# Requesting output-projection rows together, starting the SSD half earlier, and turning the SSD diagonal in a hybrid decoder layer

## The chip, the core and the metric

The kernel runs on one core of one Trainium2 chip. The metric is device microseconds of one execution; lower is better. Times before are given as the median of three runs, and one more execution was taken with the hardware profiler. The core's engines run side by side and meet at semaphores: PE multiplies matrices (its weight loads, PEld, overlap its multiplications), DVE and POOL work elementwise, ACT evaluates functions and scaled copies, and SP's queue issues the DMAs. Matrix products accumulate in PSUM, eight banks of 128 partitions by 512 floats.

## The reference

One decoder layer over 16 learned meta tokens and 1024 real tokens, width 1024, in float32. Cut to what matters here:

```python
h = concatenate([meta, x], axis=1)
proj = rms_norm(h, mix_pre_g) @ w_in                     # z, xbc, dt_raw, q, k, v
y_ssd = ssd_mixer(z, xbc, dt_raw, ...)                   # 16 heads of 64, 2 groups, chunks of 128
y_sb = rms_norm(stick_breaking_attention(q, k, v), sb_norm_g)   # 16 heads of 64, 128-query blocks
h = h + rms_norm(concatenate([y_ssd, y_sb], -1) @ w_out, mix_post_g)
gu = rms_norm(h, ffn_pre_g) @ w_up
h = h + rms_norm((gelu(causal_dwconv(gu[..., :D_FF])) * gu[..., D_FF:]) @ w_down, ffn_post_g)
return h[:, 16:]

# inside ssd_mixer, per chunk:
y_diag = einsum('bgcls,bgjcls,bcsgjp->bclgjp', CB, Ldec, Xdt)
y_off  = einsum('bclgn,bcgjpn,bgjcl->bclgjp', Cc, prev, exp(Acs))
y = (y_diag + y_off + xs * d_skip) * silu(z);  rms_norm(y, norm_g)
```

## The kernel before

Products whose operands are split are done three times: each float32 operand is written as a high part and a low part, and PE multiplies high by high, high by low and low by high into the same PSUM bank. Small products (scores, transposes, the SSD pieces, the halo) run in plain float32, and one such product shows as two matmul records in the trace; a transpose shows as one.

The stages, in order:

1. **Head.** The nine token tiles (16 meta tokens, then eight of 128) are loaded, normalised (L213) and turned through PE, eight 128x128 transposes a tile in two halves (L219), into `xh` (an ACT copy, L221) and `xl` (a DVE subtraction, L222). Both halves take their PSUM bank from one tag, `tp`, which has two buffers.
2. **First projections.** `dt` (16 columns) and the B and C blocks of group 0 run over the three column chunks `CH` (348, 346, 346 tokens) interleaved, by `project_steps` (L155 to L166). For `dt` that is 8 blocks of the contraction times 3 products a chunk. Nine transposes bring `dt` to tokens (`tpd`, L390), and a chain of some twenty DVE operations (L401 to L424) makes the decay exponents. `decays()` (L427) multiplies them on PE with triangular matrices (`pz_ea`, `pz_de`, `pz_cd`) after two steps of the following `x` projections; the B block is turned to tokens later.
3. **SSD scan.** For each of two groups, nine chunks (one of 16 tokens, eight of 128) pass through `chunk_weights`, `chunk_outputs` and `chunk_store`, between steps of the remaining projections (`fill`). In `chunk_outputs`, eight products `em` (128x128, stationary) by `xdt` (64 columns, moving), one a head, make the diagonal part `yg` in token layout (L507); DVE adds it to `yo` (L508); the part from the carried state `yf` is added; `chunk_store` turns `yo` by four transposes (L525).
4. **Attention.** For eight head pairs `p` and eight query blocks `i`, `block_weights` makes scores on PE (`z`, L596), two sigmoids on ACT (L597, L598), a scan on DVE (L601) and products on POOL (L603); `block_turn` transposes (L617) and copies (L619); `block_mix` multiplies by the values (`av`, L631), where two 64-column stationaries write the two partition halves of one bank. PE's order is as written here, by hand. `block_turn` follows three blocks behind. Between these, PE takes steps of `fill`, the q, k and v projections of the later pairs, which is used up in pair 6.
5. **Output projection, SSD half.** `wout_steps` (L701) takes the eight 128x1024 row blocks of `w_out` one by one: load into the tag `wraw` (two buffers), scaled copy to `wh` on ACT (L717), `wl` on DVE (L718), and `halo_mm`, two float32 products of the two halo tokens into 2-partition strips of one bank (strips at partitions 0 and 32 for even `k`, 64 and 96 for odd). It runs two steps a block from pair 6, block 5, to pair 7, block 1. `ssd_half` (`first`) then gives one step a half token tile, 24 products each: sixteen steps, of which pair 7 takes one each in blocks 2 to 4 and two each in blocks 5 to 7. After the last block a drain loop takes one at each round.
6. **Output projection, stick-breaking half.** `second` repeats `wout_steps` for rows 8 to 15, one step for each step left of `first` and the rest after it. Then the normalisations, the feed-forward layer and its down projection follow; after block 8 of this half everything is ordered by hand.

Where the order isn't written by hand, it comes from a scheduler that reads the program's order and dependencies. `wraw` holds 128x1024 floats in two buffers, and `whi` and `wlo` the same in three (`WB`); all three tags serve every weight that is loaded.

Of the kernel before, what the change touches and what calls it, by code (L numbers as in the profile page):

```python
# [16 lines left out]
P = 128  # L17
# [34 lines left out]
def tile_layer(ctx: ExitStack, tc: tile.TileContext, x, meta, rows, parts,  # L52
# [148 lines left out]
    with tc.tile_pool(name="pre", bufs=3, side="right") as pre:  # L201
        gpre = row_bcast(pre, 0, D, "gpre")
        for i in range(NT + 1):
# [11 lines left out]
            for hf in range(2):  # L215
                tp = psum_tp(f"xtp{i}_{hf}")
# [87 lines left out]
    with tc.tile_pool(name="ssd", bufs=1, side="right") as sp:  # L304
# [68 lines left out]
        dtT = rp.tile([16, L + 3], F32, name="dtT", tag="rt", bufs=1)  # L373

        def dt_evac(acc, c0, n):
            nc.vector.tensor_copy(dtT[:, c0:c0 + n], acc[:16, :n])

        head = [project_steps(load_w(w_dt, 16, "dt"), 16, xh, xl, CH, dt_evac, "dt")]
# [8 lines left out]
        for i in range(NT + 1):  # L387
            nr = NM if i == 0 else P
            c0 = 0 if i == 0 else NM + (i - 1) * P
            nc.tensor.transpose(tpd[:nr, i * 16:(i + 1) * 16], dtT[:, c0:c0 + nr], ident[:16, :16])  # L390
# [46 lines left out]
        run(fill, 2)  # L437
        decays()
        tmp.close()
        run(fill, 2)  # L440
        bc[0][1][0]()
# [40 lines left out]
        def chunk_outputs(g, c, em, xdt, yo, prev):  # L482
# [22 lines left out]
            yg = psum_sd(f"yd{nm}").rearrange("p (h d) -> p h d", d=64)  # L505
            for h in range(8):
                mm(yg[:nr, h, :], em[:nr, h, :nr], xdt[:nr, h, :], start=True, stop=True)  # L507
            nc.vector.tensor_tensor(yo[:nr], yg[:nr], yo[:nr], op=ALU.add)  # L508
# [9 lines left out]
        def chunk_store(g, c, yo, zk):  # L518
# [5 lines left out]
            for b in range(4):  # L524
                nc.tensor.transpose(tp[:, b, :nr], yo2[:nr, b * P:(b + 1) * P], ident[:nr, :nr])  # L525
# [14 lines left out]
        def scan_steps(g):  # L540
# [3 lines left out]
            for c in range(NT + 1):  # L544
# [4 lines left out]
                chunk_store(g, c, yo, zk)  # L549
# [151 lines left out]
    def wout_steps(pool, half, gain, res, y0, acc):  # L701
# [8 lines left out]
        for k in range(8):  # L710
            wr = wp.tile([P, D], F32, tag="wraw", name=f"wor{nm}{k}")
            r0 = (8 * half + k) * P
            nc.sync.dma_start(out=wr, in_=w_out[r0:r0 + P, :])
# [72 lines left out]
    for p in range(8):  # L786
        for i in range(NT):
# [7 lines left out]
            run(first, int(p == 7 and i > 4))  # L795
# [6 lines left out]
            if p == 6 and i == 5:  # L802
# [5 lines left out]
                wsteps = wout_steps(w1pool, 0, ssd_g, wres, halo_y(w1pool, 0, ssd_g), halo)  # L808
# [823 lines left out]
```

## Time and profile before

| | us |
|---|---|
| median of 3 runs | 1834.47 (1833.14 to 1835.4) |
| the profiled execution, its time | 1832.72 |
| the profiled execution, its span | 1831.0 |

| engine | busy, us | share of the span |
|---|---|---|
| PE | 1758.9 | 96% |
| PEld | 1508.3 | 82% |
| DVE | 1060.3 | 58% |
| POOL | 858.5 | 47% |
| ACT | 829.0 | 45% |

PE's busy time is the union of its matmul records, which overlap in the pipeline, so the price of one matmul in a stream is the distance from its start to the next start, not its duration. The granted TensorE clock over the span is 0.989 of full speed. PE is idle for 72.1 us in all; what ended those idle times is listed in the view of waits.

### The profile page before, as it was taken

The page shows a single profiled execution, that of the slowest core. Times are in us where ns is not written, and L with a number is a line of the kernel's source. Part 1 is how long each engine was busy: PE and PEld are TensorE (multiplying, and loading weights), DVE is VectorE, ACT ScalarE, POOL GpSimd, SP SyncE. Part 2 cuts the span into 40 slices and gives each one's busy share as a digit, 9 for nine tenths or more (in the row PEclk, how much of TensorE's full clock was granted, in tenths as well). Part 3 has the DMA queues.
Part 4 walks back from the last instruction along what each step waited for, and adds up shares of the span by engine and source line. Part 5 has one row for each costly group of instructions (what it writes and reads, how often), then busy time and mean ns, then how long its engine had stood idle before and what let it go on. Part 6 is the DMA issues. An engine that isn't in the chain of part 4 may idle for free.

```text
span 1831.0 us, 27362 instructions
## 1 busy us (share of the span) xinstructions
PE 1758.9 (96%) x10957; PEld 1508.3 (82%) x10957; DVE 1060.3 (58%) x1142; ACT 829.0 (45%) x1371; POOL 858.5 (47%) x613
## 2 busy tenths in 40 slices
PE   6899999999999999999799989899999999999997
PEld 5899889889888888888478767788889998888886
DVE  5551783574534544544722256766666666667988
ACT  5333454443655655655654243443333333344444
POOL 3213563485644644643764132276777776600001
PEclk9999999999999999999899999999999999999999
DMA  4123242231011110110232455233233333196344
GB/s 155 47 70 119 75 125 96 71 103 54 24 36 36 32 39 28 32 36 11 82 106 70 139 175 181 81 104 92 87 103 111 104 103 99 52 316 230 95 120 160
DMA packets 91443, 173.96 MB, mean 95 GB/s; under 512 B 11722, under 2 KB 36714, under 8 KB 91316
## 3 DMA queue, kind: packets, MB, share of 16 engines
q1 hardware_dynamic: 91316, 172.21, 29.9%
q8 instruction: 86, 1.41, 0.3%
q14 instruction: 41, 0.34, 0.1%
HBM read 122.39 MB, written 49.79 MB: 94 GB/s over the span
## 4 chain that ended last, share of the span: by engine, by line
PE 47%; DVE 3%; ACT 2%; POOL 1%; issue 1%; DMA 1%; POOLq 0%; SPq 0%; ACTq 0%; DVEq 0%
PE dn L1445 11%; PE fX L1054 9%; PE mo L759 6%; PE fY L1054 6%; PE fA L1054 6%; PE tw L617 1%; PE av L631 1%; PE z L596 1%; PE pj_v L163 1%; PE pj_q L163 1%; PE halo L708 1%; PE pj_k L163 1%; DVE oxn L912 1%; DVE mb L903 1%; POOL yl L749 0%
## 5 line engine op out<-in xcount | busy, mean ns | idle before, releaser
L601 DVE TENSOR_TENSOR_SCAN kp<-kp,hold 128x272 f32<-128x272 f32 (+7 forms) x128 | 206.7, 1657 | 202.3 <-ACT kp L597 99.6
L603 POOL TENSOR_TENSOR bt<-bt,kp 128x256 f32<-128x256 f32 (+7 forms) x128 | 213.8, 1688 | 195.9 <-DVE kp L601 143.3
L997 POOL TENSOR_TENSOR wl<-wr,wh 128x1024 fp32r<-128x1024 f32 x44 | 110.7, 2524 | 40.7 <-ACT wh L996 40.7
L1445 PE MATMUL dn<-dl,dh 128*128 128x512 f32 x308 | 120.1, 390 | 0.1
L1445 PE MATMUL dn<-dh 128*128 128x512 f32 x308 | 120.1, 390 | 0.0
L1445 PE MATMUL dn<-dh,dl 128*128 128x512 f32 x308 | 120.0, 390 | 0.0
L1491 POOL TENSOR_TENSOR fms<-fms,nhalf 128x1 f32<-128x1 f32 x8 | 8.5, 1060 | 225.8 <-DMA ar<-fda 186.0
L597 ACT ACTIVATE kp<-z 128x288 f32<-128x288 f32 (+6 forms) x112 | 82.7, 738 | 60.4 <-PE z L596 37.3
L1374 ACT ACTIVATE dh<-ar 128x512 fp32r<-128x512 f32 x77 | 48.7, 632 | 111.2 <-PE dn L1445 88.9
L996 ACT ACTIVATE wh<-wr 128x1024 fp32r<-128x1024 f32 x44 | 46.6, 1060 | 114.9 <-PE fX L1054 68.3
L596 PE MATMUL z<-k,q 64*128 64x144 f32 (+6 forms) x448 | 88.0, 494 | 8.3 <-ACT bt L598 3.9
L1126 DVE SCALAR_TENSOR_TENSOR ga<-gr,pp,ga 128x1024 f32<-128x1024 f32 x44 | 71.4, 1622 | 34.7 <-ACT ga L1119 34.0
L619 ACT ACTIVATE th<-tw 128x1024 f32<-128x1024 f32 (+2 forms) x96 | 74.4, 811 | 33.2 <-PE tw L617 31.1
L598 ACT ACTIVATE bt<-z 128x288 f32<-128x288 f32 (+6 forms) x112 | 83.0, 741 | 0.0
L617 PE MATMUL tw<-ident,bt 128*128 128x128 f32 x576 | 78.3, 282 | 4.4 <-POOL bt L603 2.9
L631 PE MATMUL av<-th,v 128*64 128x128 f32 x1152 | 78.1, 281 | 0.0
L631 PEld LDWEIGHTS av<-th,v 128*64 128x64 f32 x1152 | 62.6, 138 | 18.1 <-issue 17.3
L1375 DVE TENSOR_TENSOR dl<-ar,dh 128x512 fp32r<-128x512 f32 x77 | 53.2, 691 | 41.9 <-ACT dh L1374 41.8
L617 PEld LDWEIGHTS tw<-ident,bt 128*128 128x128 f32 x576 | 62.9, 143 | 15.9 <-issue 10.6
L596 PEld LDWEIGHTS z<-k,q 64*128 64x128 f32 x448 | 37.8, 191 | 39.0 <-issue 15.8
L1445 PEld LDWEIGHTS dn<-dh 128*128 128x128 f32 x308 | 57.8, 188 | 12.3 <-ACT dh L1374 0.3
L1445 PEld LDWEIGHTS dn<-dl,dh 128*128 128x128 f32 x308 | 57.9, 188 | 12.2 <-DVE dl L1375 0.4
(542 smaller groups left out, 5797.1 us busy)
## 6 DMA issues: line engine op xcount, KB each, us to landing
wr<-in_w_up SPq DMA_DIRECT2D x44, 512.0 KB
fds<-ga SPq DMA_DIRECT2D x44, 256.0 KB
b<-in_w_down SPq DMA_DIRECT2D x44, 256.0 KB
ar<-fds SPq DMA_DIRECT2D x44, 256.0 KB
fda<-ga SPq DMA_DIRECT2D x33, 256.0 KB
ar<-fda SPq DMA_DIRECT2D x33, 256.0 KB
yk<-yd SPq DMA_DIRECT2D x16, 512.0 KB
zd<-zt SPq DMA_DIRECT2D x8, 520.0 KB
```

The source lines that it names most:

```text
L596: mm(z[:, j, :w], q[h, t0:t0 + P], k[h, a:a + w], start=True, stop=True)
L597: nc.scalar.activation(kp[:, :, a:a + w], z[:, :, :w], AF.Sigmoid, scale=-QSCALE)
L598: nc.scalar.activation(bt[:, :, a:a + w], z[:, :, :w], AF.Sigmoid, scale=QSCALE)
L601: nc.vector.tensor_tensor_scan(kp[:, j][:, ::-1], kp[:, j][:, ::-1], hold[:, L - n:L][:, ::-1], 0.0, op0=ALU.mult, op1=ALU.max)
L603: nc.gpsimd.tensor_tensor(bt[:, j, 0:m], bt[:, j, 0:m], kp[:, j, 1:m + 1], op=ALU.mult)
L617: nc.tensor.transpose(tw[:, j, b, :], bt[:, j, c0:c0 + P], ident)
L619: nc.scalar.activation(th[:, :, :nb, :], tw[:, :, :nb, :], AF.Copy)
L631: mm(av[halves[j], :], v[:, kb, halves[j]], th[:, j, b, :], start=kb == 0, stop=kb == i)
L759: mm(acc, u[:, k, :], v[:, cs], start=(k == 0 and j == 0), stop=(k == 7 and j == 2))
L997: nc.gpsimd.tensor_tensor(l, raw, h.bitcast(F32), op=ALU.subtract)
L1054: mm(acc[:, c, :nn], u[:, k, :], v[:, k, c0:c0 + nn], start=first and k == 0 and j == 0, stop=k == 3 and j == 2, skip_group_check=not first)
L1445: mm(banks[t], u[:, 0, c], v[:, 1, :], start=(p == 0 and i == 0), stop=(p == NPR - 1 and i == 2))
```

## The change

- **Head.** The half-tile transposes take their bank in turn from the tags `tp`, `z` and `sd`, of two buffers each.
- **dt.** The high and low parts of `w_dt` lie side by side as one 32-column stationary, which is multiplied with `xh` and `xl`: 16 products a chunk for 24, and a term low by low that was left out is now included. The two halves are added by the turn to tokens, a float32 product with a 32x16 matrix of two stacked identities (`fold`).
- **decays.** It comes after four steps of `fill` and after the turn of the B block.
- **SSD diagonal turned.** `xdt` (64 columns) is now stationary and `em` (128 columns) moving, so the diagonal part comes out with the channels on the partitions, two heads in the two halves of the bank, in `chunk_store`. The four transposes of `yo` accumulate onto it, and the DVE addition L508 is gone.
- **SSD half.** All eight raw row blocks are requested in block 4 of pair 6, two into `wraw` and six into `whi` and `wlo`; `wout_steps` runs four steps in block 5 and four in block 6; `first` begins in block 7 of pair 6 and then runs in blocks 1, 3, 5, 6 and 7 of pair 7, one step each.
- **Halo.** The halo products of two consecutive row blocks are issued together.
- **Second half.** Its eight raw row blocks are requested at once, four into `wraw` and four into a tag `wr` of three buffers; two steps of `second` follow each step of `first`; the second token tile is split before the loop.
- The scratch for dynamic DMA is set to 2048.

```diff
-                tp = psum_tp(f"xtp{i}_{hf}")
+                tp = (psum_tp, psum_z, psum_sd)[(2 * i + hf) % 3](f"xtp{i}_{hf}")
...
+        dtT = rp.tile([32, L + 3], F32, name="dtT", tag="rt", bufs=1)
+        fold = sp.tile([32, 16], F32, name="fold", tag="fold")
+        nc.vector.tensor_tensor(fold, ident[:32, 0:16], ident[:32, 16:32], op=ALU.add)
+        def dt_steps():
+            raw = wp.tile([P, KB, 16], F32, tag="wraw", name="wr_dt")
+            hl = wp.tile([P, KB, 32], F32R, tag="whi", name="wh_dt", bufs=WB)
+            nc.sync.dma_start(out=raw, in_=w_dt)
+            nc.scalar.activation(hl[:, :, 0:16], raw, AF.Copy)
+            nc.gpsimd.tensor_tensor(hl[:, :, 16:32], raw, hl[:, :, 0:16].bitcast(F32), op=ALU.subtract)
+            for c0, n in CH:
+                acc = psum_mm(f"pj_dt_{c0}")
+                for k in range(KB):
+                    for j, src in enumerate((xh, xl)):
+                        mm(acc[:32, :n], hl[:, k, :], src[:, k, c0:c0 + n],
+                           start=(k == 0 and j == 0), stop=(k == KB - 1 and j == 1))
+                nc.vector.tensor_copy(dtT[:, c0:c0 + n], acc[:32, :n])
+                yield
...
-            nc.tensor.transpose(tpd[:nr, i * 16:(i + 1) * 16], dtT[:, c0:c0 + nr], ident[:16, :16])
+            mm(tpd[:nr, i * 16:(i + 1) * 16], dtT[:, c0:c0 + nr], fold, start=True, stop=True)
...
-        run(fill, 2)
+        run(fill, 4)
+        bc[0][1][0]()
         decays()
         tmp.close()
-        run(fill, 2)
-        bc[0][1][0]()
         run(fill)
...
-            yg = psum_sd(f"yd{nm}").rearrange("p (h d) -> p h d", d=64)
-            for h in range(8):
-                mm(yg[:nr, h, :], em[:nr, h, :nr], xdt[:nr, h, :], start=True, stop=True)
-            nc.vector.tensor_tensor(yo[:nr], yg[:nr], yo[:nr], op=ALU.add)
...
             for b in range(4):
-                nc.tensor.transpose(tp[:, b, :nr], yo2[:nr, b * P:(b + 1) * P], ident[:nr, :nr])
+                for j in range(2):
+                    mm(tp[halves[j], b, :nr], xdt[:nr, 2 * b + j, :], em[:nr, 2 * b + j, :nr],
+                       start=b == 0, stop=False, skip_group_check=True)
+            for b in range(4):
+                mm(tp[:, b, :nr], yo2[:nr, b * P:(b + 1) * P], ident[:nr, :nr], start=False, stop=True,
+                   is_transpose=True, skip_group_check=True)
...
         for k in range(8):
-            wr = wp.tile([P, D], F32, tag="wraw", name=f"wor{nm}{k}")
-            r0 = (8 * half + k) * P
-            nc.sync.dma_start(out=wr, in_=w_out[r0:r0 + P, :])
+            wr = raws_.pop(0) if raws_ else raw_w(half, k, None)
...
             if len(todo) > 1:
-                halo_mm(*todo.pop(0))
+                for arg in todo:
+                    halo_mm(*arg)
+                todo.clear()
             yield
-        halo_mm(*todo.pop(0))
...
-            run(first, int(p == 7 and i > 4))
+            if p == 6 and i == 4:
+                ahead = [raw_w(0, k, None if k % 3 == 0 and k < 6 else wp_f32(("wlo", "whi", "wlo")[k % 3], f"wora{k}"))
+                         for k in range(8)]
...
-            if p == 7 and i == 1:
+            if p == 6 and i == 6:
                 run(wsteps)
                 halo_store(w1pool, 0, halo)
+                ys1 = [split_y(wp, 0, 1, ("whi", "wlo", WB))]
                 first = ssd_half(wres, ys1)
-            elif p > 5:
-                run(wsteps, 2)
-            if p == 7 and i == 0:
-                ys1 = [split_y(wp, 0, 1, ("whi", "wlo", WB))]
-            run(first, int(p == 7 and i > 1))
+            elif p == 6 and i == 5:
+                run(wsteps, 4)
+            run(first, int(p == 7 and (i % 2 or i > 5) or p == 6 and i == 7))
...
+    y0b = halo_y(op, 1, sb_g)
+    ahead = [raw_w(1, k, None if k % 5 < 2 else est.tile([P, D], F32, tag="wr", name=f"worb{k}", bufs=3)) for k in range(8)]
+    second = wout_steps(op, 1, sb_g, wres2, y0b, halo, ahead)
     run(second, 1)
     ys = [split_y(op, 1, 1, ("yh", "yl", 2))]
     for _ in first:
-        run(second, 1)
+        run(second, 2)
     run(second)
+    ys.append(split_y(op, 1, 2, ("yh", "yl", 2)))
...
-        if t < NT - 1:
+        if 1 < t < NT - 1:
             ys.append(split_y(op, 1, t + 1, ("yh", "yl", 2)))
...
-    nc = bacc.Bacc("TRN2", target_bir_lowering=False, num_devices=1)
+    nc = bacc.Bacc("TRN2", target_bir_lowering=False, num_devices=1, dynamic_dma_scratch_size=2048)
```

More of the change, by code (lines that the diff above doesn't have):

```diff
@@ L371, in tile_layer @@
         nc.scalar.activation(expa, alog, AF.Exp)
[L373 to L378, printed above, removed]
+        dtT = rp.tile([32, L + 3], F32, name="dtT", tag="rt", bufs=1)
[15 more added lines that the diff above has]
+                yield
+        head = [dt_steps()]
         bc = bc_flow(0)
@@ L516, in chunk_outputs, with chunk_store @@
             return yo, zk, nprev
-        def chunk_store(g, c, yo, zk):
+        def chunk_store(g, c, em, xdt, yo, zk):
             nr = NM if c == 0 else P
@@ L699, in attend_meta, with raw_w, wp_f32, wout_steps @@
         nc.gpsimd.tensor_copy(sq[:, M0:NM], sqm[:, 0, :])
-    def wout_steps(pool, half, gain, res, y0, acc):
+    def raw_w(half, k, tile_):
+        wr = tile_ if tile_ is not None else wp.tile([P, D], F32, tag="wraw", name=f"wor{half}{k}")
+        r0 = (8 * half + k) * P
+        nc.sync.dma_start(out=wr, in_=w_out[r0:r0 + P, :])
+        return wr
+    def wp_f32(tag, name):
+        return wp.tile([P, 8, P], F32R, tag=tag, name=name, bufs=WB).bitcast(F32).rearrange("p a b -> p (a b)")
+    def wout_steps(pool, half, gain, res, y0, acc, raws_):
         nm = "ab"[half]
```

9 lines of the change are left out of this document (4 added, 5 removed).

## The prediction

> **What bounds the kernel now.** I read the page's summary first, then the busy time of stretches of the span, then PE's own waits, and last the instructions of the stretches that the change touches.
>
> ```profile
> PE 1758.9 (96%) x10957; PEld 1508.3 (82%) x10957; DVE 1060.3 (58%) x1142; ACT 829.0 (45%) x1371; POOL 858.5 (47%) x613
> ```
>
> PE is busy 96% of the 1831.0 us, so its idle time is only 72.1 us. Next, where that lies (us from the start; after the total come PE, PEld, DVE, ACT and POOL busy, the granted clock, and the DMA share).
>
> ```profile
> 0.00:50.00 50.00, 32.35 (x184) 26.79 (x185) 25.20 (x44) 24.12 (x43) 14.23 (x24) 1.00 0.43 141
> 200.00:420.00 220.00, 213.62 (x1319) 192.90 (x1318) 147.05 (x174) 109.61 (x233) 127.35 (x108) 0.99 0.32 95
> 860.00:917.60 57.60, 45.35 (x364) 27.89 (x359) 40.94 (x28) 39.86 (x63) 36.70 (x26) 0.91 0.27 82
> 917.60:1030.00 112.40, 110.64 (x651) 86.19 (x652) 24.23 (x22) 47.79 (x76) 48.85 (x33) 1.00 0.30 94
> 1030.00:1068.00 38.00, 33.74 (x151) 20.59 (x150) 15.93 (x16) 15.25 (x20) 7.63 (x3) 1.00 0.49 154
> ```
>
> The idle time lies in the head (17.6 us), between the end of the projections and the first SSD output step (12.2 us, at a granted clock of 0.91) and around the second half's weights (4.3 us). The SSD scan, 200 to 420, is full of PE work: 6.4 us idle in 220. So two kinds of edit pay here: PE work taken out where PE is full, and idle time filled where it is not. What ends the idle times (total, times, longest, in us):
>
> ```profile
> PE xtp L219 <- DVE xl L222: 6.0, 4, 2.2
> PE pz_ea L431 <- DVE s L419: 4.9, 1, 4.9
> PE z L596 <- ACT bt L598: 3.9, 2, 3.5
> ```
>
> **The change part by part.**
>
> *SSD diagonal.* Now, and what has the turned form's shape:
>
> ```profile
> 233.28 1.02 PE L496 MATMUL st<-xw,bn 128*128 128x512 f32 x2
> 234.14 1.89 PE L507 MATMUL yd<-xdt,em 128*128 128x64 f32 x16
> 235.84 0.40 PE L163 MATMUL pj_X<-xh,wh_X 128*128 128x346 f32 x1
> ...
> 966.88 1.09 PE L631 MATMUL av<-th,v 128*64 128x128 f32 x16
> 967.91 1.31 PE L617 MATMUL tw<-ident,bt 128*128 128x128 f32 x10
> ```
>
> Eight products in the old form take PE from 234.14 to 235.84, 1.70 us. The turned form has 64-column stationaries, 128 moving columns, and two partition halves in turn. That is exactly `av`, whose eight products take 966.88 to 967.91, 1.03 us. With 16 full chunks this gives 16 x 0.67 = 10.7 us; the two 16-token chunks I leave at zero. The four transposes stay. None of them accumulates in this trace; the bounds are no cost and, if each ran as two records like other float32 products, the four once more, at most their whole duration:
>
> ```profile
> 242.84 0.60 PE L525 MATMUL yt<-ident,yo 128*128 128x128 f32 x4
> L508 DVE TENSOR_TENSOR yo<-yd,yo x18: 671/678/692, 193.2 to 433.2; 128x512 f32<-128x512 f32 x16, 16x512 f32<-16x512 f32 x2
> ```
>
> 0.60 us x 16 = 9.6 us at worst. I take none, since operation, operands and sizes stay. The DVE addition that goes (18 x 0.678 = 12.2 us of DVE time) counts nothing where PE leads; at best it takes some of the stage's 6.4 us of idle. Term: -10.7, from -14 to 0.
>
> A rule of the Trainium skill speaks against this edit: "TensorE: Matmul & The Clock Gate", section "Back-to-back issue gap", prices matmuls by moving columns, 60 cycles up to 64 and 134 at 128. By that ratio the turned set would be 134/60 x 1.70 = 3.8 us, an estimate from that page, and the kernel 16 x 2.1 = 34 us slower in this stage, some 1848 in all. The `av` row already disagrees: twice the moving columns of `yd` at 0.6 of the price.
>
> *dt.*
>
> ```profile
> 58.53 0.32 PE L163 MATMUL pj_dt<-xl,wh_dt 128*16 128x346 f32 x1
> 58.69 0.32 PE L163 MATMUL pj_dt<-xh,wl_dt 128*16 128x346 f32 x1
> 66.57 0.68 PE L390 MATMUL tpd<-ident,dtT 16*16 16x16 f32 x9
> 67.17 0.42 PE L163 MATMUL pj_X<-xh,wh_X 128*128 128x348 f32 x1
> ...
> 1043.17 2.07 PE L296 MATMUL ptb<-ones,sq 128*2 128x1 f32 x18
> ```
>
> 24 products fewer at 0.16 us are 3.8 us; the stationary grows from 16 to 32 columns, which I count as free, since the moving columns are the same. Nine plain products replace nine transposes: those take 0.60 us, and nine narrow float32 products with 128-row stationaries take 2.07 us, so 1.4 us more. Term: -2.4, from -3.8 (no extra) to -0.9 (the first chunk's third, 1.3 us, already hidden by DVE's tiles, and a little more).
>
> *Head.*
>
> ```profile
> 16.63 1.94 PE L219 MATMUL xtp<-ident,xn 128*128 128x128 f32 x8 [2.19 <-DVE xl L222]
> 20.64 1.94 PE L219 MATMUL xtp<-ident,xn 128*128 128x128 f32 x8 [2.07 <-DVE xl L222]
> 18.61 1.29 DVE L213 SCALAR_TENSOR_TENSOR xn<-xt,rs_pre,gpre 128x1024 f32<-128x1024 f32 x1 [1.20 <-PE xtp L219]
> 19.81 1.28 DVE L222 TENSOR_TENSOR xl<-xtp,xh 128x512 fp32r<-128x512 f32 x2
> ```
>
> A tile takes 4.0 us (16.63 to 20.64): PE waits for both banks until DVE's `xl`, and DVE then waits 1.20 us for PE to free `xn`. With six banks the transposes no longer wait; DVE's own 1.29 + 1.28 and some small ones, say 2.8 us, is late next. Three tiles pass before PE fills up with projections: 3 x 1.2 = 3.6 us, of the 6.0 us of this wait. Term: -3.5, from -6.0 to 0 (DVE leads anyway).
>
> *decays.* PE reaches `pz_ea` 4.9 us early; two steps of 24 x 0.16 = 3.8 us were meant to lie between, and about 13 us of work did.
>
> ```profile
> 71.51 0.15 DVE L401 TENSOR_TENSOR dtx<-tpd,dtb 16x16 f32<-16x16 f32 x1
> 85.27 0.31 DVE L419 SCALAR_TENSOR_TENSOR s<-dt,expa 128x144 f32<-128x144 f32 x1
> 88.72 0.49 PE L163 MATMUL pj_X<-xh,wh_X 128*128 128x348 f32 x1
> 89.59 0.49 PE L163 MATMUL pj_X<-xh,wh_X 128*128 128x348 f32 x1
> ```
>
> DVE's chain ends 19.0 us after the start of `tpd` (66.57 to 85.58). Four steps, the B turn (about 1.2 us) and the longer fold (2.0) put 18.5 us of PE work there: about 0.5 us of stall left, 4.4 us gained. After the stall three products take 0.87 us (88.72 to 89.59) instead of 0.48, for some 3 us; without the stall that goes too, about 1 us. Term: -5.0, from -6.5 to -2.5 (the scheduler may put it earlier again).
>
> *SSD half and its halo products.*
>
> ```profile
> 900.91 1.04 PE L708 MATMUL halo<-wora,y 128*2 128x512 f32 x8
> 906.13 1.03 PE L708 MATMUL halo<-wora,y 128*2 128x512 f32 x4 [0.60 <-DMA wora<-in_w_out]
> L708 PE MATMUL halo<-worb,y 128*2 128x512 f32 x32 | 7.2, 591 | 1.8 <-POOL yl L749 1.2 <-DMA worb<-in_w_out 0.6
> L708 PE MATMUL halo<-wora,y 128*2 128x512 f32 x32 | 7.0, 702 | 0.8 <-DMA wora<-in_w_out 0.8
> 889.03 3.71 DMA wora<-in_w_out
> 927.84 5.51 PE mo L759 x24
> SPq L713 <- PE halo L708: 32.2, 7, 10.2
> 864.00:901.00 37.00, 26.66 (x175) 15.14 (x177) 29.27 (x20) 27.31 (x43) 25.53 (x14) 0.86 0.20 58
> L718 DVE SCALAR_TENSOR_TENSOR wola<-wora,pp,woha 128x1024 fp32r<-128x1024 f32 x5 | 8.7, 1731 | 4.0 <-ACT woha L717 4.0
> ```
>
> Two row blocks in four strips cost 1.04 us, the price of one in two strips (1.03), so the strips run side by side. Eight blocks cost 7.0 us now and 4 x 1.04 = 4.2 in pairs: -2.8. The requests now wait 32.2 us on SP for `wraw`, and a row (3.71 us) then ends waits; with eight buffers, free by the end of the projections near 864, it does not. PE's idle time there has other causes too: the chain of ACT, DVE and POOL on bare blocks. DVE is busy 29.27 of 37 us in blocks 3 to 7 of pair 6 with five `wl`; eight add 3 x 1.73 = 5.2 us, 34.5 of 37, and ACT gets three more copies: DVE is late next, and I charge 2 us. One step of `first` (24 products, 5.5 us) then lies in block 7 and one in pair 7's block 1, and later blocks of pair 7 lose four of nine: blocks 0, 2 and 4 go bare, which I charge 1.5 us, against 1.8 us idle there now. Filling the early holes returns perhaps 3.7 of the 12.2 us. Term: -2.8 + 2 + 1.5 - 3.7 = -3.0, from -17 (all idle and clock loss of that stretch) to +9.
>
> *Second half.* It has the same halo saving, 7.2 us to 4.2, -3.0. Five steps of `first` (27 us) now cover eight rows at 3.7 us each and the split, where two did; the 4.3 us idle goes except 1.3. On SP, rows 5, 6 and 7 wait for a buffer, and the yk load and the stores of `first` are queued behind; the first pair frees `wraw` one step in, 5.5 us, and the second split is asked for before its use. Term: -6.0, from -7.3 to -1.
>
> The rest, normalisations, feed-forward and tails, has the same instructions and moves as a block; the scratch size counts nothing, because every data transfer is on a queue issued by SP. Sum: -10.7 - 2.4 - 3.5 - 5.0 - 3.0 - 6.0 = -30.6. The profiled execution took 1832.7, so 1802.1; the median lies 1.8 above it, so I give **1803**.
>
> **The rivals.**
>
> *The steps fill the whole hole.* All idle and clock loss of 860 to 917.6 (12.2 + 0.09 x 57.6 = 17.4 us) goes, 14 beyond my net 3: 1789. For it: ACT and DVE are near 70% there. Against: they and POOL wait on each other, and DVE gets more.
>
> *Bare blocks.* Blocks 0, 2 and 4 of pair 7 behave as blocks 3 to 7 of pair 6 do: 10.3 us idle and 0.14 x 37 = 5.2 us of clock over five blocks, so 9.3 for three, +9: 1812. For it: the same engines. Against: the small blocks have less to wait for. Part 1 of the same page says that an idle window of about 3.4 us halves the clock; the 0.86 row agrees.
>
> *The column halves follow each other.* Priced by `st`, 0.86 us (233.28 to 234.14) for two records of 512 columns, 16 records of 128 take 1.72 us; the diagonal gains nothing: 1814. Against: the `av` row.
>
> *Requests stay late*, so the change does not do what it says: SP holds the rows as now, and terms five and six go: 1812. Against: the buffers are free.
>
> *Slower.* In the turned form each record's price doubles with its moving columns: 1.70 to 3.40 us in the SSD scan, where nothing hides it. That is +27.2 in place of -10.7: 1841. It decides from a set of 2.95 us (19.9 us of other gains over 16 chunks). Against it, `av` at 1.03 with the same shapes; for it, only that the operands differ. The page rule above is this rival.
>
> **How the numbers follow.** Forecast 0.53; hole filled 0.13; bare blocks 0.17; halves in turn 0.08; requests late 0.04; slower 0.05. The range 1788 to 1816 takes in all but the slower case and the tails of the terms. A difference of 0.2% (3.7 us) is what a measurement can tell. Faster 0.93, same 0.02, slower 0.05.
>
> **What would show it.** Right: sixteen diagonal records in about 1.03 us and no L508; 48 `dt` products; no wait of `xtp` on `xl` and under 1 us at `pz_ea`; halo groups of eight records, four a half; no wait of `halo` or `mo` between the last block and the normalisations; pair 7 with 3 us idle or less. Wrong: a diagonal set near 1.7 or 3.4 us, or pair 7 with over 10 us idle or a granted clock under 0.9.

## The result, and the profile after

The changed kernel takes 1810.33 us (median of 4 runs, 1809.65 to 1811.43) against 1834.93 us (4 runs) for the kernel before beside it: a ratio of 0.9867, 95% interval 0.985 to 0.9884. That is 24.6 us faster; 31 were forecast, to 1803. The profiled execution has a span of 1809.0 us, 22.0 less than before.

The summary of the profile after, in the columns of the one before:

```profile
PE 1734.8 (96%) x10942; PEld 1490.1 (82%) x10942; DVE 1061.0 (59%) x1125; ACT 831.3 (46%) x1373; POOL 863.3 (48%) x613
```

PE's busy time fell by 24.1 us and its idle time rose, from 72.1 to 74.2. So the change took work out of PE, as planned; it did not fill holes. Where holes are now (total, times, longest, in us):

```profile
PE xtp L221 <- DVE ms_pre L188: 11.4, 1, 11.4
PE xtp L221 <- DVE xn L213: 6.5, 4, 4.3
PE z L612 <- ACT bt L614: 6.0, 3, 4.7
...
PE mo L783 <- ACT yh L772: 4.3, 1, 4.3
PE z L612 <- DVE thc L659: 4.1, 7, 2.3
PE tt_B L331 <- DVE bn L327: 2.9, 1, 2.9
...
PE mo L783 <- POOL yl L773: 2.4, 2, 1.7
...
PE halo L733 <- DMA worb<-in_w_out: 1.8, 1, 1.8
...
PE pz_ea L447 <- DVE s L435: 1.0, 1, 1.0
```

The wait of `xtp` on `xl` (6.0 before) has become one of 6.5 on `xn`; the 4.9 at `pz_ea` shrank to 1.0, with 2.9 new at the turn of B. `mo <- yh` grew from 0.9 to one wait of 4.3, `z <- bt` from 3.9 to 6.0 and `z <- thc` from 2.0 to 4.1. The stretches after, in the columns of before (head, scan, blocks 3 to 7 of pair 6, pair 7, the second half's rows):

```profile
0.00:50.00 50.00, 32.16 (x190) 29.53 (x191) 25.88 (x45) 24.03 (x44) 13.70 (x24) 0.93 0.42 142
200.00:420.00 220.00, 214.98 (x1415) 189.11 (x1415) 151.73 (x160) 110.83 (x231) 135.69 (x114) 1.00 0.33 98
841.00:885.00 44.00, 33.14 (x220) 20.26 (x218) 41.17 (x24) 36.00 (x57) 32.80 (x16) 0.92 0.23 73
885.00:985.00 100.00, 92.93 (x646) 71.53 (x644) 27.98 (x25) 44.51 (x72) 48.37 (x38) 0.98 0.18 57
985.00:1035.00 50.00, 42.24 (x187) 29.64 (x185) 12.62 (x13) 21.27 (x28) 11.91 (x5) 0.90 0.56 190
```

In the last blocks of pair 6 (841 to 885) DVE works 41.2 of 44 us and PE 33.1. Around the second half's rows PE is idle 7.8 us of 50 at a clock of 0.90.

To see where the time came from, the span is cut at six marks: the first `sg` (the scan begins), the last `yt` (it ends), the last `pj_v` (the projections end), the last `avc` (the attention ends), the first `x2tp` (the normalisations begin) and the last `dn`. Steps of `first` were moved past the last `avc`, three of them; at 5.5 us a step (the row of 24 `mo` records shown with the prediction) the table counts all kernels as if nine steps lay before it.

| stretch, us | before | after | difference | forecast |
|---|---|---|---|---|
| start to first `sg` (head, dt, decays) | 176.0 | 169.5 | -6.5 | -10.9 |
| to last `yt` (scan, diagonal) | 262.4 | 248.3 | -14.1 | -10.7 |
| to last `pj_v` | 425.2 | 423.6 | -1.6 | 0 |
| to last `avc` (attention, SSD half) | 158.6 | 144.1 + 16.5 | +2.0 | -3.0 |
| to first `x2tp` (second half) | 59.7 | 78.9 - 16.5 | +2.7 | -6.0 |
| to last `dn` (all the rest) | 738.6 | 734.1 | -4.5 | 0 |

The first three parts together gave 22.2 us where 21.6 were forecast, but not part by part: the head gave 4.4 less, the scan 3.4 more, and 1.6 came where nothing was changed. The two parts of the output projection, forecast at -9.0, cost 4.7.

Part of this scatter is the clock. Read in slices of 1 us, the granted clock is 1.00 or 0.50, but for the few slices that hold an edge between the two. The time at half clock in the six stretches is 6.8, 3.4, 3.4, 10.3, 0.0 and 10.3 us before and 13.6, 0.0, 0.0, 10.2, 10.2 and 3.4 after: always a multiple of some 3.4 us. Such a window of 3.4 us costs up to 1.7 us, and less where PE is idle in it. PE's idle time in the six is 24.1, 6.4, 1.5, 14.0, 4.3 and 11.8 us before and 21.8, 5.0, 1.5, 17.9, 8.2 and 9.7 after. So the -1.6 is one window, and the +2.0 of the attention is 3.9 us more idle time against less work. Up to the last `dn` the two executions are alike, 34.2 and 37.4 us at half clock.

What is behind the +2.7 stands in the timeline of the changed kernel around 1000 us (start, duration, engine, line; in brackets the idle time before and what ended it):

```profile
990.53 1.38 SPq L720 DMA_DIRECT2D worb<-in_w_out  x3
...
994.18 0.80 SPq L720 DMA_DIRECT2D wor<-in_w_out  x2
...
999.26 0.33 SPq L720 DMA_DIRECT2D worb<-in_w_out  x1
...
999.63 0.90 SPq L771 DMA_DIRECT2D yk<-yd  x2
...
1006.92 1.06 ACT L772 ACTIVATE yh<-yk 128x1024 fp32r<-128x1024 f32 x1 [0.46 <-DMA yk<-yd]
1008.03 1.22 PE L783 MATMUL mo<-woha,yh 128*128 128x512 f32 x2 [4.27 <-ACT yh L772]
...
1010.94 0.79 PE L783 MATMUL mo<-woha,yl 128*128 128x512 f32 x1 [1.69 <-POOL yl L773]
```

SP issues in order. Its last row waits until 999.26 for a buffer that the halo products free, and only then go out two loads `yk`, among them that of token tile 7, which the SSD half needs next; `yh` is made at 1006.92, and PE stands until 1008.03 and again until 1010.94. The theory for the experiments was therefore: the diagonal, `dt` and the head give what they give alone; the second half's loss is the order on SP's queue; the SSD half's is DVE, full where eight `wl` are now packed into blocks 5 and 6 of pair 6, and the bare blocks of pair 7. The rivals: transfers that collide for bandwidth, DVE that is busy but not late, and bare blocks alone.

### The profile page after: what moved, and what is told of

It is laid out like the page before. It is cut to its first block, busy times and chain, and to the rows that moved or that the text cites. A ratio compares the mean times of both kernels' runs of the same rounds, so it can differ in the third digit from the quotient of the medians.

```text
span 1809.0 us, 27308 instructions
## 1 busy us (share of the span) xinstructions
PE 1734.8 (96%) x10942; PEld 1490.1 (82%) x10942; DVE 1061.0 (59%) x1125; ACT 831.3 (46%) x1373; POOL 863.3 (48%) x613
## 5 line engine op out<-in xcount | busy, mean ns | idle before, releaser
L1516 POOL TENSOR_TENSOR fms<-fms,nhalf 128x1 f32<-128x1 f32 x8 | 8.5, 1060 | 225.7 <-DMA ar<-fda 186.0
L613 ACT ACTIVATE kp<-z 128x288 f32<-128x288 f32 (+6 forms) x112 | 82.8, 739 | 56.8 <-PE z L612 33.1
L1021 ACT ACTIVATE wh<-wr 128x1024 fp32r<-128x1024 f32 x44 | 46.6, 1060 | 114.7 <-PE fX L1079 68.3
L647 PEld LDWEIGHTS av<-th,v 128*64 128x64 f32 x1152 | 62.8, 138 | 18.8 <-issue 17.9
```

The costliest lines, as they stand in the source:

```text
L613: nc.scalar.activation(kp[:, :, a:a + w], z[:, :, :w], AF.Sigmoid, scale=-QSCALE)
L647: mm(av[halves[j], :], v[:, kb, halves[j]], th[:, j, b, :], start=kb == 0, stop=kb == i)
```

## The experiments

Each kernel was timed against the kernel before on the same chip. The last four columns are the stretches of the table above, in one profiled execution each (us).

| kernel | median, us | ratio to before (95%) | to `pj_v` | to `avc` | to `x2tp` | to `dn` |
|---|---|---|---|---|---|---|
| before | | 1 | 863.6 | 158.6 | 59.7 | 738.6 |
| the changed kernel | 1810.33 | 0.9867 (0.985 to 0.9884) | 841.4 | 160.6 | 62.4 | 734.1 |
| p1_diag | 1820.37 | 0.9931 (0.9911 to 0.9951) | 847.5 | 159.0 | 60.2 | 737.9 |
| p2_head | 1833.59 | 0.9992 (0.9981 to 1.0002) | 861.7 | 159.2 | 61.9 | 737.6 |
| p3_dtdec | 1831.89 | 0.9994 (0.998 to 1.0008) | 857.4 | 160.2 | 62.6 | 738.6 |
| p4_wout | 1833.64 | 0.9994 (0.9983 to 1.0005) | 861.7 | 160.6 | 63.4 | 733.6 |
| a1_second_old | 1806.79 | 0.9845 (0.9832 to 0.9858) | 841.5 | 160.6 | 57.0 | 735.4 |
| a2_y8_first | 1801.49 | 0.9817 (0.9803 to 0.983) | 839.3 | 162.1 | 53.1 | 734.6 |
| a6_y7_first | 1801.75 | 0.9832 (0.9814 to 0.9851) | 843.0 | 160.6 | 53.1 | 735.0 |
| a3_timetable_old | 1809.96 | 0.9861 (0.9848 to 0.9875) | 843.5 | 163.0 | 53.4 | 737.9 |
| a4_spread | 1801.54 | 0.9815 (0.9801 to 0.9828) | 842.2 | 159.0 | 54.4 | 733.7 |
| a5_spread_y8 | 1802.43 | 0.9835 (0.9815 to 0.9854) | 840.1 | 158.6 | 54.0 | 733.7 |
| a7_wl_twice | 1816.49 | 0.9912 (0.9897 to 0.9927) | 840.1 | 167.1 | 62.7 | 734.1 |
| a8_rows_only | 1808.21 | 0.987 (0.9851 to 0.9889) | 839.8 | 167.8 | 57.7 | 734.5 |

The profiled executions of p1 and a5 are the fastest of their kernels' runs (1817.12 and 1798.63 us), that of a8 is the slowest (1812.07). The columns vary without an edit too: the nine kernels that are the same up to the last `pj_v` reach it at 839.3 to 843.5 us.

**One part of the change alone.** p1 is the kernel before with the turned diagonal (the hunks of `chunk_outputs` and `chunk_store`):

```diff
-            for h in range(8):
-                mm(yg[:nr, h, :], em[:nr, h, :nr], xdt[:nr, h, :], start=True, stop=True)
...
+                    mm(tp[halves[j], b, :nr], xdt[:nr, 2 * b + j, :], em[:nr, 2 * b + j, :nr],
+                       start=b == 0, stop=False, skip_group_check=True)
```

> The kernel before with the turned SSD diagonal alone. The theory that the matmuls' own price decides: the group of 288 diagonal records goes from 32.4 us busy to about 18.8 as in the changed kernel, nothing else of note changes, and the kernel is 13 to 15 us faster, 1820 to 1822. The theory of the prediction's sum (0.67 us for each of 16 full chunks): 10.7 us faster, 1824. The rival that the column halves follow each other: no gain, 1833 to 1836.

p2 has only the three bank tags of the head (the hunk at L215), p3 only the packed `dt` and the late decays (the hunks from `dtT` to `fill`), p4 all edits of the output projection and no other.

> The kernel before with the head's banks taken in turn from three tags, alone. The prediction's term: 3.5 us faster, 1831. The rival that DVE leads anyway: the waits of the transposes on xl become waits on xn, and the gain is 0 to 1.5 us, 1833 to 1835.

> The kernel before with the packed dt products and the later decays, without the head's banks. The prediction's two terms: 2.4 + 5.0 = 7.4 us faster, 1827. What the stages of the changed kernel suggest (the start of the SSD scan 6.5 us earlier, the head included): 5 to 6 us faster, 1829, with the wait at pz_ea down from 4.9 to about 1 us and a new wait of the B turn of about 3 us.

> The kernel before with the output projection's edits alone (rows requested together, SSD half early, halo products in pairs, second half's rows at once, scratch size). The prediction's terms: 9 us faster, 1826. The theory formed from the changed kernel's trace: the halo pairs gain about 6 us of PE time and the stage gives it all back, in blocks 3 to 7 of pair 6, where DVE is full, in the bare blocks of pair 7, and in a wait of the SSD half for its last token tile behind the second half's rows; 0 to 2 us faster, 1833 to 1835. The rival that the parts hinder each other: 4 us or more faster alone.

The diagonal alone is 1 - 0.9931 of 1835, 12.7 us (9 to 16), and its scan, from the first `sg` to the last `yt`, is 248.3 us long in both kernels that have it. The output projection alone is no gain at all, with the waits of the changed kernel: that settles that its two terms failed by themselves, not by meeting the other edits. The head and the `dt` edits bring the end of the projections forward by 1.9 and 6.2 us (p4, whose edits lie behind that mark, also reaches it 1.9 us earlier, so the 1.9 shows nothing; the head's own mark, the first `tpd`, comes 2.5 us earlier), and yet the intervals of both ratios hold no change. In p2 the place is seen. The kernel before, then p2, between 1060 and 1070:

```profile
1060.00:1070.00 10.00, 7.50 (x31) 4.84 (x28) 2.69 (x3) 5.08 (x11) 2.35 (x1) 1.00 0.49 155
```

```profile
1060.00:1070.00 10.00, 7.25 (x19) 5.19 (x18) 1.41 (x2) 4.92 (x9) 3.89 (x2) 0.66 0.46 136
```

PE is idle for nearly the same time, 2.5 and 2.75 us, with waits for the same `yl` and `yh`, but in p2 the granted clock is 0.50 from 1063.1 to 1070.0 where it was 1.00. That is up to 3.4 us lost, and the stretch to `x2tp` is 2.2 us longer, nearly all that the head had won. It isn't one execution alone: the mean granted clock is 0.9859 over the ten runs of p2 and 0.9865 over the ten of p3, against 0.9876 over the 25 of the kernel before beside them, which is 3.1 and 2.0 us of the span. So nearly the same hole costs more or less by where it falls.

By their ratios the four parts alone give 12.7, 1.5, 1.1 and 1.1 us, 16.4 together, where the whole gives 24.4. Whether the other 8 us are clock or edits that help each other isn't settled.

**The second half's rows.** a1 asks for them one by one again (`ahead` is replaced by an empty list). a2 asks for a split before the rows:

```diff
+    ys1.append(split_y(wp, 0, NT, ("whi", "wlo", WB)))
     wres2 = []
...
-            if t < NT:
+            if t < NT - 1:
                 ys.append(split_y(wp, 0, t + 1, ("whi", "wlo", WB)))
```

> The changed kernel, but the second half's eight raw rows are requested one by one as they are used (pairs and everything else stay). Theory (in the changed kernel the last token tile of the SSD half, split t = 8, is queued on SP behind the second half's rows, so yk lands near 1005, ACT's yh and POOL's yl follow, PE waits 4.3 + 1.7 us at mo and its clock drops to 0.79 in 995 to 1012): with late requests yk is issued earlier, the waits of mo on yh and yl shrink to under 2 us together, but halo waits for worb rows more (over 5 us instead of 1.8); between two steps per block of rows the net is within 3 us of the changed kernel, 1807 to 1813. Rival (asking for all rows at once is what the second half gains from): over 3 us slower, 1814 or more, by waits of halo on worb.

> The changed kernel, but the split of the last token tile of the SSD half is issued before the second half's rows are requested. Theory (order on SP's queue): the waits mo <- ACT yh 4.3 and mo <- POOL yl 2.4 go (under 1 us together), the clock of 995 to 1012 returns from 0.79 to over 0.95, and the span from the end of the averages to the last SSD step shrinks by 6 to 8 us: 1802 to 1805. Rival (bandwidth: the rows themselves, 250 GB/s in that window, are what is late): yk lands as late as now or the rows land later in its place, halo <- worb grows by the same amount, 1808 to 1812.

At that place tile 7's split had not been asked for either. So a2 takes tile 8's split for tile 7's step and the other way round, and its output has those two tiles exchanged; the work is the same. It came out at 1801.49, as the order on the queue says. a6 repeats it with each tile in its own step (tile 7 before the rows, tile 8 one tile ahead).

> The changed kernel, with the split of token tile 7 issued before the second half's rows are requested and that of tile 8 one tile ahead of its use, so each tile is used for its own tokens (the earlier run that asked for tile 8 first had exchanged tiles 7 and 8). Theory (order on SP's queue is the whole loss of the second half): as that run, 1800 to 1804, x2tp starts 69 to 71 us after the last avc instead of 78.9, no wait of mo on yh. Rival (the exchange, not the order, gave the gain): 1807 to 1811.

In a6 the load goes out first (timeline, then the stretch of the second half's rows):

```profile
991.68 0.32 SPq L771 DMA_DIRECT2D yk<-yd  x1
...
992.55 1.37 SPq L720 DMA_DIRECT2D worb<-in_w_out  x3
...
995.13 1.06 ACT L772 ACTIVATE yh<-yk 128x1024 fp32r<-128x1024 f32 x1 [0.72 <-DMA yk<-yd]
```

```profile
985.00:1035.00 50.00, 49.59 (x232) 36.25 (x231) 12.78 (x15) 21.56 (x28) 14.32 (x6) 0.97 0.68 227
```

`yh` is ready 12 us earlier, PE works 49.6 of 50 us there instead of 42.2, and the stretch to `x2tp` falls from 62.4 to 53.1. In the same 50 us the DMA engines move 227 GB/s instead of 190, so bandwidth was not what was late. a1 stands between, with 57.0: the old requests are better than the new ones in the wrong order (its median's distance, 1806.8 to 1810.3, is at the edge of the intervals), and all at once in the right order is better still.

**The timetable.** a3 has the steps where they were before; a4 spreads the rows, two a block from block 5 of pair 6 to block 0 of pair 7, with a step of `first` in each of blocks 1 to 7; a8 is a4 with those steps in blocks 1, 3, 5, 6 and 7 only; a5 is a4 with tile 8's split before the second half's rows. The edit of a4:

```diff
-            if p == 6 and i == 6:
+            if p == 7 and i == 0:
...
-            elif p == 6 and i == 5:
-                run(wsteps, 4)
-            run(first, int(p == 7 and (i % 2 or i > 5) or p == 6 and i == 7))
+            elif p > 5:
+                run(wsteps, 2)
+            run(first, int(p == 7 and i > 0))
```

> The changed kernel, but with the old timetable of steps: two row steps per block from block 5 of pair 6 to block 1 of pair 7, one step of the first half in blocks 2 to 4 and two in blocks 5 to 7 of pair 7; the rows are still requested together. Theory (DVE, full in blocks 3 to 7 of pair 6, 37.0 of 38.6 us, pays back what the early rows give; and blocks 0, 2 and 4 of pair 7 are bare): z <- ACT bt falls from 6.0 to under 3, z <- DVE thc from 4.1 to under 2, and the stretch from the end of the projections to the end of the averages is shorter after allowing 5.5 us for each step of the first half that lies in another place; 1804 to 1808. Rival (starting the half in block 7 of pair 6 does gain, by filling holes): 3 us or more slower, 1813 to 1817, with PE idle in blocks 5 to 7 of pair 6 at 12 us or more.

> The changed kernel, but the eight row steps are spread, two per block in blocks 5, 6 and 7 of pair 6 and two in block 0 of pair 7, and one step of the first half in each of blocks 1 to 7 of pair 7, so no block is bare. Theory: the longest wait z <- bt 4.7 in block 7 of pair 6 goes, the thc wait of 2.3 too, the clock of blocks 3 to 7 of pair 6 rises from 0.91; 3 to 5 us faster, 1805 to 1807. Rival (what is paid there is DVE's total work, not its crowding, or bare blocks cost nothing): within 2 us of the changed kernel, 1808 to 1812.

> The spread timetable, but the steps of the first half lie in blocks 1, 3, 5, 6 and 7 of pair 7, so blocks 2 and 4 carry none (two steps more come after the attention). Theory (bare blocks cost little; what the spread gains is DVE's crowding): from the end of the projections to the last avc 137 us, that is the 148.0 of the spread timetable less two steps of 5.5, within 1 us; total 1801 to 1804. Rival (a bare block costs some 3 us as the rival of the prediction said, 9.3 for three): 140 us or more for that stretch, with waits of z on thc or bt of 2 us and more in blocks 2 and 4 of pair 7.

> The spread timetable (two row steps per block from block 5 of pair 6 to block 0 of pair 7, one step of the first half in blocks 1 to 7 of pair 7) with the split of token tile 8 issued before the second half's rows. Theory: the spread timetable already asks for tile 7 before the rows, so only tile 8's split is left to gain: 0 to 2 us under the spread timetable alone, 1799 to 1802. Rival (the gains of the two edits are separate and add): 1794 to 1797.

The expectation of a3 missed: its attention is 2.4 us longer than the changed kernel's, not shorter. The two waits that were to shrink did, `z <- bt` to 2.2 us and `z <- thc` to 2.1, but `z <- th` on ACT grew from 2.5 to 7.5, with one wait of 6.2 at 897.8. Its `first` is past tile 7 when the rows are asked for, which is worth 9.0 us up to `x2tp` (62.4 to 53.4), but what follows takes 3.8 us longer, and so does the start by 2.1, where the code is the same and two windows at half clock fall into the scan. a4 gained more than expected for the same reason: 8.0 of the 9.2 us between the two profiled spans lie in the second half, where it too has asked for tile 7 in time, and 1.6 in the attention. So a5 has little left to gain and shows none that its interval can tell. a8 missed on the other side: two blocks without a step cost 8.8 us in the profiled executions. Most of pair 7 in a4, then in a8:

```profile
885.00:985.00 100.00, 93.80 (x596) 72.58 (x595) 28.68 (x24) 44.39 (x73) 50.33 (x39) 0.97 0.22 68
```

```profile
885.00:985.00 100.00, 92.44 (x565) 70.22 (x563) 25.59 (x23) 42.37 (x70) 45.55 (x36) 0.90 0.18 60
```

Here PE is idle only 1.4 us more, and the clock is 0.90 against 0.97. Over the whole stretch from the last `pj_v` to the last `avc`, PE is idle 20.5 us in a8 and 16.5 in a4, and at half clock for 20.5 and 10.2: 4.0 us of the 8.8 are idle time and some 5 the clock. That is a8's slowest execution; by ratio it is 6 us slower than a5, which ran on the same chip (0.987 to 0.9835). The changed kernel leaves blocks 0, 2 and 4 bare too: its pair 7 is idle 3.4 us more than that of the kernel before (7.1 to 3.7) and has one window of 3.4 us at half clock. So a bare block has no fixed price: it leaves PE some idle time, and whether the clock falls too differs from one timetable to the next.

**DVE.** a7 is the changed kernel with the eight `wl` of the SSD half made twice each, to the same result:

```diff
+            for _ in range(2 - half):
-            nc.vector.scalar_tensor_tensor(wl, wr, gk, wh.bitcast(F32), op0=ALU.mult, op1=ALU.subtract)
+                nc.vector.scalar_tensor_tensor(wl, wr, gk, wh.bitcast(F32), op0=ALU.mult, op1=ALU.subtract)
```

> The changed kernel with the eight DVE operations that make the low halves wl of the SSD half's rows done twice each, with the same result; nothing else. Theory (DVE is what is late in blocks 5 and 6 of pair 6: 37.0 of 38.6 us busy): eight more operations of 1.3 to 2.5 us, most of them on the path: 6 to 14 us slower than the changed kernel, 1816 to 1824, by waits of z on thc and bt. Rival (DVE is busy but not late; ACT and POOL and their waits on each other set those blocks): under 3 us slower, 1809 to 1813.

It takes 6.5 us more in the attention and about 6 in all (1816.49; by ratio, 0.9912 to 0.9867, 8 us). More work on DVE there is thus paid for, 0.8 us for each of the eight operations. But the waits are not those expected: `z <- bt` and `z <- thc` are unchanged at 6.0 and 4.0 us. In a7's timeline:

```profile
874.12 13.62 DVE L742 SCALAR_TENSOR_TENSOR wola<-wora,pp,woha 128x1024 fp32r<-128x1024 f32 x7
...
879.62 3.33 POOL L774 TENSOR_TENSOR yl<-yk,yh 128x1024 fp32r<-128x1024 f32 x1
...
883.01 0.79 PE L784 MATMUL mo<-woha,yl 128*128 128x512 f32 x1 [4.40 <-POOL yl L774]
...
887.66 8.74 DVE L617 TENSOR_TENSOR_SCAN kp<-kp,hold 128x1040 f32<-128x1040 f32 x4
```

Seven `wl` in a row stand before the scan of block 7, whose start moves from 877.48 to 887.66. POOL's `yl` comes later too, and PE waits for it 4.4 us where it waited 0.7; the rest is mostly clock, 0.83 where the changed kernel's row has 0.92, 4 us of 44:

```profile
841.00:885.00 44.00, 29.39 (x195) 16.68 (x192) 43.63 (x28) 35.74 (x56) 30.26 (x14) 0.83 0.20 67
```

So it isn't DVE that PE waits for in the longest wait of the changed kernel's attention, 4.7 us, which a7 has unchanged. PE waits there for the first sigmoids of block 7 of pair 6, and what comes before them on ACT is:

```profile
866.14 2.23 ACT L740 ACTIVATE woha<-wora,pp 128x1024 fp32r<-128x1024 f32 x2
868.22 1.56 ACT L761 ACTIVATE mh<-halo 2x256 f32<-2x256 f32 x4
869.80 1.06 ACT L772 ACTIVATE yh<-yk 128x1024 fp32r<-128x1024 f32 x1
870.88 0.75 ACT L613 ACTIVATE kp<-z 128x696 f32<-128x696 f32 x1
...
872.32 1.52 PE L612 MATMUL z<-k,q 64*128 64x344 f32 x4 [4.72 <-ACT bt L614]
```

Two copies of rows, four of the halo and one of `yh` take ACT 4.7 us before it comes to the scores that PE began to write at 866.16. In a4 the copies of the halo and `yh` come later, ACT starts those sigmoids at 867.97, and the wait is 1.9 us; its eight `wl` stand on DVE in the same order, 0.8 us later than in the changed kernel. So what a4 eases there is ACT's order, and DVE's load is as it was.

## Why the prediction was right, and where it was wrong

The time lay in the range and the sign was right, because the terms where PE's own work goes were sound in the stretches where they lie. Two of the six terms failed, and that the total comes as near as it does is in part luck: 6.1 us (1.6 and 4.5) came from stretches whose instructions the change leaves alone. (1802.1 and 1.8 make 1803.9, not the 1803 that was given; nothing hangs on it.)

**Diagonal (forecast -10.7, measured -14.1).** The mechanism and the price were right. Eight products of the changed kernel, then its transposes:

```profile
200.96 1.09 PE L537 MATMUL yt<-em,xdt 128*64 128x128 f32 x16
...
201.98 0.66 PE L540 MATMUL yt<-ident,yo 128*128 128x128 f32 x4
```

From 200.96 to 201.98 are 1.02 us, where 1.03 was read off `av`; the 3.40 us of the slower rival are out. The four accumulating transposes nearly kept their price, but now wait for DVE's `yo`, as the groups say (line, busy, mean in ns; the kernel before had 10.6 us, which follows as the second fence):

```profile
L537 PE MATMUL yt<-em,xdt 128*64 128x128 f32 (+1 forms) x288 | 18.8, 271 | 0.0
L540 PE MATMUL yt<-ident,yo 128*128 128x128 f32 (+1 forms) x72 | 11.4, 279 | 2.8 <-DVE yo L526 2.7
```

```profile
L507 PE MATMUL yd<-xdt,em 128*128 128x64 f32 (+1 forms) x288 | 32.4, 266 | 0.5 <-DVE em L472 0.5
L525 PE MATMUL yt<-ident,yo 128*128 128x128 f32 (+1 forms) x72 | 10.6, 269 | 0.0
```

PE's own work in the stretch fell by 11.0 us, as good as forecast. The other 3.1 are PE's idle time, which fell from 6.4 to 5.0 us, and one window at half clock, 1.7 us, which the scan had before and no longer has. Both are the same in p1. That the DVE addition that went is the reason for the idle time isn't shown.

**Head, dt, decays (-10.9; measured -6.5, and -7.5 to -9.4 in the eight experiments with the same front).** Alone, the head gave 2.5 us at the first `tpd` (3.5 forecast), since `xtp` now waits for `xn`: DVE is what is late next, as said, but by more. `dt` gave 2.2 by the first `pj_X` after it (67.2 to 65.0; 2.4 forecast) and the decays about 4.0 by the first `sg` (5.0 forecast): the wait at `pz_ea` fell to 1.0, about as said, and the B turn put ahead of it, for which no wait was counted, waits 2.9 for DVE's `bn`. The changed kernel's profile shows less still because its first tile came 1.1 us later (11.4 instead of 10.3 at `ms_pre`) and its first 50 us ran at 0.93; up to the first `sg` it was at half clock for 13.6 us, the kernel before for 6.8. None of this shows in the total of p2 or p3.

**SSD half (-3.0; measured +2.0).** The halo pairs cost what was said, eight records in 1.04 us. The steps that failed are "filling the early holes returns perhaps 3.7 of the 12.2 us" and the 1.5 us for the bare blocks, and "DVE is late next" named the wrong engine for the longest wait. Block by block, PE is idle 10.3 us in blocks 3 to 7 of pair 6 before and 10.9 after, so nothing was filled: the rows came early, but ACT's copies stood before the sigmoids (the 4.7 us above, where 3.5 was the longest). Pair 7 up to the last `avc` was idle 3.7 us and is idle 7.1, and it got a window at half clock, together some 5 us; its longest wait, 2.3 us at 905.97, is for `thc`, which on DVE stands behind the scan of bare block 2. The early blocks have one window at half clock less. DVE, put at 34.5 of 37 us, reached 41.2 of 44, since its `wl` did not keep their price:

```profile
L741 DVE SCALAR_TENSOR_TENSOR wola<-wora,pp,woha 128x1024 fp32r<-128x1024 f32 x6 | 13.3, 2246 | 0.2 <-ACT woha L740 0.2
...
L741 DVE SCALAR_TENSOR_TENSOR wolb<-worb,pp,wohb 128x1024 fp32r<-128x1024 f32 x4 | 5.1, 1284 | 3.2 <-ACT wohb L740 3.1
```

Six of the eight in the attention took 2246 ns each and two 1892, where 1731 was read, and the same operation took 1284 in the second half. a7 shows that still more work on DVE there would be paid for in time; it does not show that the eight as they are cost any. How the +2.0 splits between ACT's order, DVE and the bare blocks isn't settled beyond these waits: a4, which eases ACT's order and leaves no block bare, gets back 1.6.

**Second half (-6.0; measured +2.7).** The failed step is the sentence that the `yk` load and the stores "are queued behind; the first pair frees `wraw` one step in, 5.5 us, and the second split is asked for before its use". It named the queue and gave it no price. The rows stood on SP for 9.1 us (990.53 to 999.63) with tile 7's load behind them, and PE paid 4.3 + 1.7 us of waits, 1.8 for the last row, and a clock at half from 1005.0 to 1015.2, three windows, which these slices hold:

```profile
1000.00:1010.00 10.00, 3.18 (x14) 0.59 (x6) 3.77 (x3) 5.76 (x9) 3.80 (x2) 0.75 0.66 216
1010.00:1020.00 10.00, 9.06 (x31) 7.33 (x32) 0.00 (x0) 3.58 (x6) 5.71 (x3) 0.74 0.70 258
```

With one load moved ahead of the rows (a6) the stretch is 6.6 us shorter than before, so the term itself was right: what was wrong is the order in which the change puts the requests.

**The rest (0; measured -4.5).** Every kernel with a new timetable shows it (733.6 to 735.4), and a3 with the old one does not (737.9). Part of it is a wait, before and after:

```profile
PE x2tp L918 <- DVE ms_mo L188: 3.9, 1, 3.9
```

```profile
PE x2tp L943 <- DVE ms_mo L188: 1.2, 1, 1.2
```

PE's idle time in this stretch is 9.1 to 10.2 us in the nine kernels with a new timetable and 11.1 to 12.4 in the others, so some 2 us go with the timetable, and "moves as a block" was wrong there, for once to the good. That the steps which now come after the attention give DVE's chain of the normalisations more room is a likely reason, not a shown one. The rest of the -4.5 is clock, 10.3 us at half before and 3.4 after, and that is not the timetable's alone: a1, with the new one, has 10.3 too.

**The rivals.** "Bare blocks" gave 1812, next to the time that came. Its mechanism is there in part: pair 7 lost some 5 us of the 9.3, at a clock of 0.98. The other loss, in the second half, it didn't name, so its number is luck. "Requests stay late" gave 1812 as well; the requests came early, and in the second half that was the harm. Of what would show the steps right, the sixteen records in 1.03 us, the halo groups of eight and the `xtp` and `pz_ea` waits came as said (`pz_ea` at 1.0); no wait of `mo` after the last block and 3 us of idle in pair 7 did not (7.1 in 885 to 985).

A version that beats both is a4: 1801.54 us, ratio 0.9815 (0.9801 to 0.9828); the intervals of a6 and a5 overlap its own, so the three can't be told apart.

## What to carry to other kernels

When loads are asked for early on an in-order queue, list what the queue must issue next and who needs it: a request that waits for a buffer holds back every load behind it, and one load issued before the block of requests was worth 9.3 us of its stretch here and 6 to 9 us in all (a6 and a2, by ratio). The work that left PE where PE was full, in the scan, came out at its price per instruction. Work that is moved to fill a hole must be checked on every engine that carries it, for its order as well as its load: here copies on ACT came before the sigmoids that PE waited for, and DVE, busy for 41.2 of 44 us, had no room for more (a7). A gain of 2 to 6 us far from the end can be lost again before it arrives (p2 and p3), so measure such an edit at a mark close behind it, and count the time at half clock on both sides.

## What the runs showed of the hardware that was not expected

The granted clock in these traces is full or half, and the half comes in windows of some 3.4 us. In slices of 10 us that shows as values such as 0.83 and 0.66, one and two windows in the slice, and as others where a window is cut by the slice's edge. Two slices of the changed kernel:

```profile
860.00:870.00 10.00, 6.38 (x54) 2.91 (x50) 10.00 (x6) 9.90 (x16) 7.78 (x5) 1.00 0.24 87
870.00:880.00 10.00, 6.96 (x38) 5.38 (x39) 10.00 (x5) 8.32 (x15) 9.77 (x4) 0.66 0.00 0
```

PE stands from 867.6 to 872.3, the wait of 4.7 us, half in each slice. The clock is still 1.00 for the first 4.3 us of it, falls to 0.50 at 871.9 and returns at 878.7, 6.8 us later, so the price is paid by the work behind the hole. A window is 1.7 us of lost clock, which is what 3.4 us at half speed make. The Trainium skill, "TensorE: Matmul & The Clock Gate", section "What's actually happening", says that the clock has two values only, half and full, judged in windows of about 3.4 us that run freely; the slices agree, and free-running windows would explain why nearly the same hole cost nothing in the kernel before and two windows in p2. No run here moved a hole against the windows to show it.

The two column halves of a bank run side by side for plain float32 products, 16 records of 128 columns in 1.02 us, where one after the other they would take the 1.72 that the prediction read off `st`; and transposes accumulate on them at nearly their old price (11.4 us for 72, 10.6 before). And a DVE operation of one shape took 1284 ns in one stage and 2246 in another. One by one in the changed kernel, the first `wl` of the attention took 1.28 us while POOL stood idle (843.24), and those that ran beside POOL's products took 1.85 to 2.79. The last started at 876.3, just before POOL's `yl` at 876.42, and took 1.27; that `yl` took 3.35 us where others take 2.4. So the price goes with what POOL does at the time; no run was made to try it.
